# A mixture-of-experts inference step: blocks of gates issued every 1.875 steps instead of every 2

## The chip, the cores and the metric

The kernel runs on one core of one Trainium2 chip. The metric is the device time of one execution in microseconds, taken as the median of several runs.

## What is computed

One inference step of a small two-layer encoder, for 256 prompt rows and 128 sample rows of width 1024 (three tiles of 128 rows). Layer 0 mixes with a state-space block, layer 1 with windowed attention; behind each stands the same expert layer ("PEER"), and that layer is what the change touches:

```python
def block_fn(xb):                                  # 128 rows
    q = (xb @ w_q).reshape(128, 8, 256)            # 8 heads
    s1, s2 = q[..., :128] @ sub_k1.T, q[..., 128:] @ sub_k2.T
    # top 16 of each, top 16 of the sums: 128 experts a row, of 128 * 128
    eid  = e1 * 128 + e2
    gate = softmax(vs)
    act  = gelu(einsum('tkd,td->tk', u_tab[eid], xb))
    return einsum('tk,tkd->td', gate * act, v_tab[eid])
```

## The kernel before, in words

**The expert layer, dense for the prompt.** `peer(l)` runs twice, for layers 0 and 1. For the 256 prompt rows it doesn't fetch experts one by one. It multiplies the rows by all 128 x 128 experts, 128 at a time: `u_step(e2)` loads one tile of 128 experts, multiplies it with the rows into a PSUM bank, and ScalarE (ACT) writes the gelu of that into `G[e2 // 64][:, e2 % 64]`. `G[0]` and `G[1]` are the two halves of the experts' activations, 64 tiles of 128 x 256 numbers each. After 64 + 64 of these U steps come 128 V steps: `v_step(e2)` loads one tile of `p_v`, splits tile `e2` of `G`, and adds the product to four PSUM banks that stay open for all 128 steps. Full precision is made from pairs: `split` writes a rounded `hi` (a cast on ACT, L108) and the rest `lo` (a subtraction on VectorE, DVE, L109), and three matrix products replace one (L144 to L146 for U, L157 for V). For a V step the split of `G` has the names `phi` and `plo`. Some steps use the raw tile instead (L1199, L1246).

**Blocks of gates.** Before V may read a half of `G`, that half must be multiplied by the gates, which are nonzero only for chosen experts. `w_step(hf, t0)` (L1207) does it for 8 prompt rows and one half, all 64 tiles at once: DVE builds `ob` (L1212) and `og` (L1215); one tile `oa` is built by ACT (four L1225 and one L1226) and a second `oa` by DVE (L1228); TensorE (PE) multiplies 16 small matrices into a bank (L1232), 8 with the first `oa` and 8 with the second; DVE multiplies the half of `G` by that bank (L1234). 32 blocks make a half. Since each block touches every tile of its half, the first V step of a half needs all 32 blocks of it. `ob` and `og` have one buffer each, `oa` has two.

**Sample rows.** For the 128 sample rows the chosen experts are fetched: GpSimd (POOL) gathers rows of `p_u` into `gath`, DVE reduces each against the input (L1173, "U item"), and later PE multiplies gathered rows of `p_v` by small tiles `cm` (L1184 on DVE, L1190 on PE: a "quad", 8 matrix products of four gathered rows, 16 instructions in the profile).

**Order of the work.** Three loops of `peer` write the program down: 64 U steps of half 0; then 64 U steps of half 1 with the 32 blocks of half 0 among them; then 128 V steps, with the 32 blocks of half 1 among the first 64 of them. `tick` and `quads` add the U items and the quads by tables of due steps. The program is then put in order by a scheduler at build time, which fixes one sequence for each engine: an engine runs its sequence strictly in that order, and a semaphore wait holds up all that stands behind it. So the place where a line stands in the loops is a wish, and the built sequence decides. Casts of `hi` use a ring of two buffers, in the V steps of three (the third has the names `hix` and `lox`); a cast waits until PE has read the old contents of its buffer.

Of the kernel before, what the change touches and what calls it, by code (L numbers as in the profile page):

```python
# [61 lines left out]
def encoder_step(ctx: ExitStack, tc: tile.TileContext, t_in, t_out):  # L62
# [150 lines left out]
    def open_h():  # L213
        hold["pool"] = tc.tile_pool(name="resid", bufs=1, side="right")
        hold["h"] = T(hold["pool"].__enter__(), [P, NB, D], F32, tag="h")
        return hold["h"]
# [671 lines left out]
    def peer(l):  # L888
        with ExitStack() as c:
# [9 lines left out]
            HE = NKEY // 2  # L899
# [49 lines left out]
            def load_group(g):  # L949

                if g % 2:
                    xg[g] = (G[1][:, HE - 4:] if g == 1 else G[0][:, 32:36]).rearrange("p e t -> p (e t)")
                else:
                    xg[g] = T(one, [P, D], F32, tag="xg", bufs=1)
                rows = xrow[g].rearrange("c r d -> (c r) d")
                for q in range(GR):
                    pool.dma_start(xg[g][q * TG:(q + 1) * TG], rows)
# [236 lines left out]
            def u_step(e2):  # L1194
                ps = bank([P, NP])
                if e2 in NATIVE:
                    raw = load_raw(t_in["u_t"][l, e2])
                    for k in range(KD):
                        pe.matmul(ps, raw[:, k * P:(k + 1) * P], xf[:, k], start=(k == 0), stop=(k == KD - 1))  # L1199
                else:  # L1200
                    gemm_cols(ps, load_split(t_in["u_t"][l, e2]), xs[0], xs[1], 0, NP)
                act.activation(G[e2 // HE][:, e2 % HE], ps, AF.Gelu_apprx_tanh)
# [58 lines left out]
            def tick(s):  # L1261

                s0, n0 = start[0], 0
                for s1, n1 in U_DUE:
                    if s < s1:
                        break
                    s0, n0 = s1, n1
                want = P if s >= U_DUE[-1][0] else n0 + (n1 - n0) * (s + 1 - s0) // (s1 - s0)
                while done["u"] < want:
                    fetch_u(done["u"] + 2)  # L1270
                    u_item(done["u"])
                    done["u"] += 1
                    if due and due[0][0] <= done["u"]:
                        group_end(*due.pop()[1:])
                if due and done["u"] == P:
                    group_end(*due.pop()[1:])

            def quads(s):

                while done["v"] < 32 and V_DUE[done["v"]] <= s:  # L1280
                    v_quad(done["v"])
                    done["v"] += 1
                if s >= 2 * HE - 20 and done["f"] == 4 * V_FIRST and s < 2 * HE + 17:
                    return
                last = 4 * V_FIRST if s < 2 * HE else P
                ahead = 4 * done["v"] + (4 if s < 2 * HE else v_bufs(s))
                for _ in range(2):
                    if done["f"] < min(ahead, last):
                        fetch_v(done["f"], s)
                        done["f"] += 1  # L1290

            busy = True
            xs = [qhi, qlo]
            lent = tc.tile_pool(name="pe0", bufs=1)
# [34 lines left out]
            for e2 in range(HE):  # L1329
                u_step(HE + e2)  # L1330
                tick(HE + e2)
                if e2 % 2 == 1:
                    w_step(0, 8 * (e2 // 2))
                if e2 >= 7:
                    quads(HE + e2)
            xpool.__exit__(None, None, None)
# [4 lines left out]
            for e2 in range(2 * HE):  # L1341
                v_step(e2)
                if e2 == 35:
                    load_group(3)
                tick(2 * HE + e2)
                if e2 < HE and e2 % 2 == 1:
                    w_step(1, 8 * (e2 // 2))
                quads(2 * HE + e2)
                if e2 == 2 * HE - 7:
                    more.clear()  # L1350
                    lent.__exit__(None, None, None)
                    h = open_h()
                    pool.dma_start(h, spill)
# [16 lines left out]

    mamba(t_in["x"].rearrange("(b p) d -> p b d", p=P))
    peer(0)
    attention()
    peer(1)
    final()

# [95 lines left out]
```

## Time and profile before

| what | value |
|---|---|
| three runs | median 2511.06 us (2501.7 to 2518.12) |
| profiled execution, its own time | 2491.53 us |
| its span | 2489.0 us |
| PE busy | 2408.8 us, 97% of the span |
| DVE busy | 1883.5 us, 76% |
| ACT busy | 1244.5 us, 50% |
| mean granted TensorE clock | 0.99 |

Times in a trace count from the start of the span. The four places of this document are the ends of halves: in layer 0 the U steps of half 1 run from about 653 to 899 us and the V steps of half 0 from there to about 1137 us, in layer 1 from 1775 to 2018 and on to 2258 us. In a row of the timeline stand the start, the length, the engine, the line, the operation, output and inputs and the number of merged instructions, and in brackets the engine's idle time before it with what ended it. Matrix products overlap: the time that one takes from PE is the distance between two starts, not its length.

### The profile page before, as it was taken

The page shows a single profiled execution, that of the slowest core. Times are in us where ns is not written, and L with a number is a line of the kernel's source. Part 1 is how long each engine was busy: PE and PEld are TensorE (multiplying, and loading weights), DVE is VectorE, ACT ScalarE, POOL GpSimd, SP SyncE. Part 2 cuts the span into 40 slices and gives each one's busy share as a digit, 9 for nine tenths or more (in the row PEclk, how much of TensorE's full clock was granted, in tenths as well). Part 3 has the DMA queues.
Part 4 walks back from the last instruction along what each step waited for, and adds up shares of the span by engine and source line. Part 5 has one row for each costly group of instructions (what it writes and reads, how often), then busy time and mean ns, then how long its engine had stood idle before and what let it go on. Part 6 is the DMA issues. An engine that isn't in the chain of part 4 may idle for free.

```text
span 2489.0 us, 44541 instructions
## 1 busy us (share of the span) xinstructions
PE 2408.8 (97%) x16655; PEld 2017.4 (81%) x16656; DVE 1883.5 (76%) x4163; ACT 1244.5 (50%) x2406; POOL 727.3 (29%) x779
## 2 busy tenths in 40 slices
PE   8999999999999999999999998999999999999998
PEld 7899978999999986656666778999999986656676
DVE  5888846979988888777655675979988888777655
ACT  5656524433466665554344554433466665554343
POOL 2222200013334224446432100013334234346431
PEclk9999999999999999999999999999999999999999
DMA  5455434467789889989996424467799889989995
GB/s 198 169 183 180 163 125 145 143 234 253 277 313 350 297 299 342 328 323 392 363 339 201 142 69 162 137 229 262 274 311 355 297 299 343 328 325 388 362 336 206
DMA packets 177080, 649.76 MB, mean 261 GB/s; under 512 B 21136, under 2 KB 23040, under 8 KB 174208
## 3 DMA queue, kind: packets, MB, share of 16 engines
q1 hardware_dynamic: 99936, 365.85, 41.2%
q0 software_dynamic: 76928, 281.07, 31.5%
q8 instruction: 130, 2.13, 0.3%
q14 instruction: 86, 0.70, 0.1%
HBM read 630.62 MB, written 18.06 MB: 261 GB/s over the span
## 4 chain that ended last, share of the span: by engine, by line
PE 77%; DVE 4%; ACT 2%; issue 1%; DMA 1%; POOL 0%; POOLq 0%; ACTq 0%; DVEq 0%
PE bank L157 26%; PE bank L146 11%; PE bank L144 11%; PE bank L145 10%; PE bank L1190 5%; PE bank L1199 5%; PE bank L1246 3%; PE bank L1232 2%; DVE lo L109 2%; ACT hi L108 1%; DVE gath L1173 1%; PE bank L984 0%; PE bank L983 0%; DMA h<-hd 0%; PE bank L794 0%
## 5 line engine op out<-in xcount | busy, mean ns | idle before, releaser
L108 ACT CAST hi<-raw 128x1024 fp32r<-128x1024 f32 (+1 forms) x479 | 498.2, 1042 | 521.6 <-PE bank L145 380.6
L109 DVE TENSOR_TENSOR lo<-raw,hi 128x1024 fp32r<-128x1024 f32 (+1 forms) x479 | 581.8, 1216 | 193.8 <-ACT hi L108 192.2
L1133 POOL DMA_INDIRECT gath<-in_p_u,eidU x256 | 314.0, 1227 | 874.2 <-DVE gath L1173 468.6
L146 PE MATMUL bank<-xhi,lo 128*128 128x256 f32 (+1 forms) x1344 | 404.3, 301 | 6.4 <-DVE lo L109 6.4
L144 PE MATMUL bank<-xhi,hi 128*128 128x256 f32 (+1 forms) x1344 | 402.3, 300 | 0.0
L145 PE MATMUL bank<-xlo,hi 128*128 128x256 f32 (+1 forms) x1344 | 396.9, 295 | 0.0
L1133 POOL DMA_INDIRECT G<-in_p_v,eidT x256 | 290.7, 1135 | 303.4 <-PE bank L1190 220.6
L108 ACT CAST phi<-G 128x256 fp32r<-128x256 f32 x232 | 93.6, 406 | 362.1 <-PE bank L157 340.4
L146 PEld LDWEIGHTS bank<-xhi,lo 128*128 128x128 f32 x1344 | 253.8, 189 | 15.0 <-DVE lo L109 7.8
L144 PEld LDWEIGHTS bank<-xhi,hi 128*128 128x128 f32 x1344 | 253.8, 189 | 12.5 <-issue 6.9
L145 PEld LDWEIGHTS bank<-xlo,hi 128*128 128x128 f32 x1344 | 253.8, 189 | 0.3
L144 PE MATMUL bank<-qhi,hi 128*128 128x256 f32 (+1 forms) x792 | 243.9, 308 | 8.8 <-ACT xf L930 7.2
L146 PE MATMUL bank<-qhi,lo 128*128 128x256 f32 (+1 forms) x792 | 238.5, 301 | 1.9 <-DVE lo L109 1.9
L145 PE MATMUL bank<-qlo,hi 128*128 128x256 f32 (+1 forms) x792 | 238.6, 302 | 0.0
L109 DVE TENSOR_TENSOR plo<-G,phi 128x256 fp32r<-128x256 f32 x232 | 98.0, 424 | 163.1 <-PE bank L157 161.3
L157 PE MATMUL bank<-hi,phi 128*128 128x512 f32 x640 | 202.8, 412 | 13.7 <-ACT hi L108 7.9
L157 PE MATMUL bank<-lo,phi 128*128 128x512 f32 x640 | 204.9, 400 | 4.6 <-DVE lo L109 4.2
L157 PE MATMUL bank<-hi,plo 128*128 128x512 f32 x640 | 200.9, 395 | 0.0
L1225 ACT ACTIVATE oa<-ioh,e2T 128x128 f16<-128x128 f16 x512 | 163.6, 392 | 71.2 <-PE bank L1232 70.7
L157 PEld LDWEIGHTS bank<-hi,phi 128*128 128x128 f32 x640 | 117.2, 190 | 74.5 <-ACT hi L108 21.9
L1173 DVE SCALAR_TENSOR_TENSOR gath<-gath,xg 128x1024 f32<-128x1024 f32 x128 | 155.7, 1216 | 9.6 <-DMA gath<-in_p_u,eidU 9.6
L1173 DVE SCALAR_TENSOR_TENSOR gath<-gath,G 128x1024 f32<-128x1024 f32 x128 | 155.8, 1220 | 8.9 <-DMA gath<-in_p_u,eidU 8.8
(361 smaller groups left out, 4918.4 us busy)
## 6 DMA issues: line engine op xcount, KB each, us to landing
raw<-in_u_t SPq DMA_DIRECT2D x256, 512.0 KB
raw<-in_p_v SPq DMA_DIRECT2D x256, 512.0 KB
raw<-in_w_in SPq DMA_DIRECT2D x32, 512.0 KB
raw<-in_p_w_q SPq DMA_DIRECT2D x32, 512.0 KB
raw<-in_w_z SPq DMA_DIRECT2D x16, 512.0 KB
s<-in_state_ssm SPq DMA_DIRECT2D x8, 1024.0 KB
out_sm_ssm<-s SPq DMA_DIRECT2D x8, 1024.0 KB
raw<-in_w_out SPq DMA_DIRECT2D x16, 512.0 KB
```

What stands on the lines that cost most here:

```text
L108: act.copy(hi, raw)
L109: dve.tensor_tensor(lo, raw, hi32, op=OP.subtract)
L144: pe.matmul(ps, whi[:, s], xhi[:, k, c0:c1], start=(k == 0), stop=False)
L145: pe.matmul(ps, whi[:, s], xlo[:, k, c0:c1], start=False, stop=False)
L146: pe.matmul(ps, wlo[:, s], xhi[:, k, c0:c1], start=False, stop=(k == KD - 1))
L157: mm = pe.matmul(ps, x, w[:, hf * n:(hf + 1) * n], start=s_, stop=e_)
L1133: pool.indirect_dma_start(out=tile_, out_offset=None, in_=tab, in_offset=bass.IndirectOffsetOnAxis(ap=idx, axis=0))
L1173: pin(dve.scalar_tensor_tensor(tile_, tile_, 1.0, xg[g], op0=OP.mult, op1=OP.mult, accum_out=au[g][:, j:j + 1]))
L1190: pin(pe.matmul(out_s[hf][32 * q:32 * q + 32, :], cm[:, q], rows[q][:, hf * 512:hf * 512 + 512], start=(r == 0), stop=(r == 31), tile_posi ...
L1199: pe.matmul(ps, raw[:, k * P:(k + 1) * P], xf[:, k], start=(k == 0), stop=(k == KD - 1))
L1225: act.activation(a[:, i], ioh, AF.Square, scale=-1.0, bias=e2T[:, t, 0:1])
L1246: pe.matmul(accs[b][hf], G[e2 // HE][:, e2 % HE, b * P:(b + 1) * P], raw[:, hf * 512:hf * 512 + 512], start=False, stop=False)
```

## The change

The blocks stood at every second step: block i at step 2i + 1 of its 64 steps, the last at step 63. Now block i stands at step 1 + floor(1.875 i): 1, 2, 4, 6, 8, 10, 12, 14, 16, 17, 19, and so on to 55, 57, 59. The last block of half 0 so stands four U steps earlier, that of half 1 four V steps earlier. No instruction is added or taken away.

```diff
+            w_at = {1 + (60 * i) // 32: 8 * i for i in range(32)}
             busy = True
...
             for e2 in range(HE):
                 u_step(HE + e2)
                 tick(HE + e2)
-                if e2 % 2 == 1:
-                    w_step(0, 8 * (e2 // 2))
+                if e2 in w_at:
+                    w_step(0, w_at[e2])
...
                 tick(2 * HE + e2)
-                if e2 < HE and e2 % 2 == 1:
-                    w_step(1, 8 * (e2 // 2))
+                if e2 in w_at:
+                    w_step(1, w_at[e2])
                 quads(2 * HE + e2)
```

What the scheduler made of it is shown for three places of layer 0. In layer 1 the same sequences stand.

**PE, at the end of half 1's blocks.** `oa` numbers tell the blocks apart, L157 is a V step, L1190 a quad. Between two rows shown stand further instructions of the same block or quad only. Before:

```order
L157 MATMUL bank_10548<-hi_12949,plo_12954 128x512
L1232 LDWEIGHTS oa_12806
...
L1190 MATMUL bank_7292<-G_620_3971,cm_12831 32x512 x4
L1232 LDWEIGHTS oa_12897
...
L1232 LDWEIGHTS oa_12977
...
L157 MATMUL bank_10545<-hi_13004,phi_13008 128x512
```

And now:

```order
L157 MATMUL bank_10548<-hi_12979,plo_12984 128x512
L1232 LDWEIGHTS oa_12482
...
L1232 LDWEIGHTS oa_12571
...
L1232 LDWEIGHTS oa_12637
...
L1232 LDWEIGHTS oa_12714
...
L1190 MATMUL bank_7292<-G_620_3971,cm_12739 32x512 x4
L1232 LDWEIGHTS oa_12805
...
L1232 LDWEIGHTS oa_12866
...
L1190 MATMUL bank_7292<-G_620_3971,cm_12891 32x512 x4
L157 MATMUL bank_10545<-hi_13004,phi_13008 128x512
```

Before, blocks 30, 31 and 32 and one quad stood between the last V product of half 0 (`plo_12954`) and the first of half 1 (`phi_13008`). Now blocks 27 to 32 and two quads stand there: three blocks and a quad have moved behind the last V step of half 0.

**DVE, in the same place, now.** `ob`, `og`, `oa` and `G` are the parts of blocks, L109 `lo` belongs to a V step of half 1, L1173 is a U item.

```order
L1234 SCALAR_TENSOR_TENSOR G_1193_7286<-bank_12477,G_1193_7286 128x64x8
L1215 TENSOR_TENSOR og_12569<-ob_12567,g_617_3965 128x1024
L1228 TENSOR_TENSOR oa_12585<-ioh_76,e2T_3964 128x512
L109 TENSOR_TENSOR lo_13064<-raw_13061,hi_13063 128x1024
L1212 TENSOR_TENSOR ob_12633<-ioh_76,e1T_3963 128x512
L1234 SCALAR_TENSOR_TENSOR G_1193_7286<-bank_12566,G_1193_7286 128x64x8
L1215 TENSOR_TENSOR og_12635<-ob_12633,g_617_3965 128x1024
L1228 TENSOR_TENSOR oa_12651<-ioh_76,e2T_3964 128x512
L1173 SCALAR_TENSOR_TENSOR gath_12925,au_12185<-gath_12925,G_620_3971 128x1024
L1212 TENSOR_TENSOR ob_12710<-ioh_76,e1T_3963 128x512
```

So one `lo` stands between the parts of blocks 28 and 29, one U item between those of 29 and 30; in the same way another U item (L1173) stands between the G of block 31 and the `og` of block 32, all of it now behind the last V step on PE. On ACT a cast, `hi_13063`, stands ahead of the `oa` of block 28.

**ACT, at the end of half 0's blocks.** Here `hi_10573` is the cast for V step 1, L1202 the gelu of the last U step, `phi_10555` the first split of V step 0. Before:

```order
L1225 ACTIVATE oa_10601<-ioh_76,e2T_3964 128x128 x4
L1226 ACTIVATE oa_10601<-oa_10601 128x512
L108 CAST hi_10573<-raw_10571 128x1024
L1202 ACTIVATE G_1193_7286<-bank_10473 128x256
L108 CAST phi_10555<-G_620_3971 128x256
```

And now:

```order
L108 CAST hi_10551<-raw_10549 128x1024
L1202 ACTIVATE G_1193_7286<-bank_10468 128x256
L108 CAST hi_10573<-raw_10571 128x1024
L1202 ACTIVATE G_1193_7286<-bank_10503 128x256
L108 CAST phi_10555<-G_620_3971 128x256
```

The parts of a block have gone from the rows above; the last three rows stand as before.

## Prediction

> **What bounds the kernel now.** I read the page's first and fourth parts, then the busy times by stage, then PE's waits, then the timeline at the four ends of halves, then the granted clock there.
>
> ```profile
> PE 2408.8 (97%) x16655; PEld 2017.4 (81%) x16656; DVE 1883.5 (76%) x4163; ACT 1244.5 (50%) x2406; POOL 727.3 (29%) x779
> PE 77%; DVE 4%; ACT 2%; issue 1%; DMA 1%; POOL 0%; POOLq 0%; ACTq 0%; DVEq 0%
> core 0: us, PE busy (x) PEld busy (x) DVE busy (x) ACT busy (x) POOL busy (x), PEclk, DMA share, GB/s
> 653.00:899.00 246.00, 243.39 (x2359) 228.43 (x2357) 209.23 (x329) 159.09 (x316) 87.23 (x81) 1.00 0.89 312
> 899.00:1137.03 238.03, 230.83 (x1401) 153.93 (x1401) 188.50 (x321) 131.84 (x265) 103.83 (x89) 1.00 0.90 328
> ```
>
> PE is the bound: 97% busy, 77% of the chain that ended last. So this change, which leaves every instruction in place, can act only through PE's idle time and clock. The last two rows are the two stages with blocks of layer 0: PE idles 2.6 of 246 us in the first and 7.2 of 238 in the second. Those of layer 1 are their twins. This is what PE waits for in the second (line, what it waited for, us, times, longest):
>
> ```profile
> PE bank L157 <- ACT phi L108: 3.0, 2, 1.6
> PE bank L1232 <- ACT oa L1226: 1.9, 1, 1.9
> PE bank L157 <- ACT hi L108: 1.0, 1, 1.0
> PE bank L1232 <- DVE og L1215: 0.8, 2, 0.5
> ```
>
> Two waits on `phi` open the two halves of V, and the 1.9 us on `oa` is a wait between the last two blocks. So something does stand still at both ends of halves; the question is what.
>
> **End of half 0: removes nothing.**
>
> ```profile
> 898.71 0.28 PE L146 MATMUL bank<-xhi,lo 128*128 128x256 f32 x1
> 900.58 0.73 PE L157 MATMUL bank<-hi,phi 128*128 128x512 f32 x2 [1.59 <-ACT phi L108]
> 896.84 0.69 DVE L1234 SCALAR_TENSOR_TENSOR G<-bank,G 128x512 f32<-128x512 f32 x1
> 898.91 1.04 ACT L108 CAST hi<-raw 128x1024 fp32r<-128x1024 f32 x1 [0.26 <-PE bank L145]
> 899.86 0.38 ACT L1202 ACTIVATE G<-bank 128x256 f32<-128x256 f32 x1
> 900.14 0.70 ACT L108 CAST phi<-G 128x256 fp32r<-128x256 f32 x2
> ```
>
> The last block had multiplied `G` by 897.5, 1.2 us before PE even finished its last U step. PE then idles 1.59 us for `phi`, and `phi` is late because ACT has a cast and a gelu ahead of it, and the cast waits for PE (L145) to let go of a `hi` buffer. In the changed sequence cast, gelu and `phi` stand in the same order. Moving the blocks forward doesn't touch this: 0 us, bounds 0 (same order) to a gain of 1.6 us a layer (if `phi` were free).
>
> Inside the U stage the blocks now come at 1 or 2 steps' distance. DVE was busy 209.2 of 246 us there and does about 1.9 us for a block (steps of 0.34, 0.60, 0.60 and 0.34 us between starts, as in the rows below); 32 blocks in 60 steps instead of 64 leave it under 90%. A late `lo` cost PE no more than the 2.6 us of all its idle time in that stage. I take 0, bounds -1 to +2 us a layer.
>
> **End of half 1: the tail grows.** Layer 0, then layer 1:
>
> ```profile
> 1129.67 0.64 PE L1232 MATMUL bank<-og,oa 128*128 128x64 f16 x16
> 1130.24 1.92 PE L1190 MATMUL bank<-G,cm 128*32 128x512 f32 x16
> 1132.51 0.63 PE L1232 MATMUL bank<-og,oa 128*128 128x64 f16 x16 [0.34 <-DVE og L1215]
> 1135.00 0.64 PE L1232 MATMUL bank<-og,oa 128*128 128x64 f16 x16 [1.86 <-ACT oa L1226]
> 1137.03 1.22 PE L157 MATMUL bank<-hi,phi 128*128 128x512 f32 x2 [1.39 <-ACT phi L108]
> 1133.00 1.28 ACT L1225 ACTIVATE oa<-ioh,e2T 128x128 f16<-128x128 f16 x4
> 1132.02 1.03 ACT L108 CAST hi<-raw 128x1024 fp32r<-128x1024 f32 x1
> 1133.17 0.69 DVE L1234 SCALAR_TENSOR_TENSOR G<-bank,G 128x512 f32<-128x512 f32 x1 [0.26 <-PE bank L1232]
> 1133.78 0.68 DVE L1215 TENSOR_TENSOR og<-ob,g 128x1024 f16<-128x1024 f16 x1
> 1134.38 0.42 DVE L1228 TENSOR_TENSOR oa<-ioh,e2T 128x512 f16<-128x512 f16 x1
> 1134.71 1.22 DVE L109 TENSOR_TENSOR lo<-raw,hi 128x1024 fp32r<-128x1024 f32 x1
> 1135.85 0.69 DVE L1234 SCALAR_TENSOR_TENSOR G<-bank,G 128x512 f32<-128x512 f32 x1
> ...
> 2256.41 0.94 PE L1232 MATMUL bank<-og,oa 128*128 128x64 f16 x16 [1.86 <-ACT oa L1226]
> 2258.57 1.22 PE L157 MATMUL bank<-hi,phi 128*128 128x512 f32 x2 [1.22 <-ACT phi L108]
> ```
>
> Blocks 30, 31, 32 and a quad run here with no V step between: 7.36 us from 1129.67 to 1137.03. Two neighbouring blocks cannot come closer than a chain: PE reads the first `oa`; 0.49 us after the block's start ACT begins the next one (1132.51 to 1133.00); 2.00 us later PE starts (1135.00). Period 2.49 us, of which PE works 0.57 (1129.67 to 1130.24). A V step between two blocks would hide it.
>
> In the built sequence the change does the opposite of its wish: six blocks, 27 to 32, and two quads now stand behind half 0's last V step. Counting from block 27's start, with the sequences shown:
>
> - 27 to 28: ACT first casts `hi_13063`, whose buffer PE frees only with that last V step: about 0.1 us, 0.98 for the cast (1132.02 to 1133.00), 2.00 for `oa`: 3.1 us.
> - 28 to 29: ACT's chain, 2.5 us (DVE's `lo` of 1.14 us just fits).
> - 29 to 30: DVE's chain. After its `oa` for block 28, at 2.3 us, it must do `lo` 1.14, `ob` 0.34, G 0.60, `og` 0.60, `oa` 0.33, a U item 1.15, `ob` 0.34, G 0.60, `oa` 0.33, `og` 0.60: 8.4 us; block 30 starts then, 2.85 after block 29.
> - 30 to 31: 2.5, the quad between is covered.
> - 31 to 32: G 0.66 us after the block's start, 0.61, the U item 1.15, `og` 0.60, `oa` 0.42: 3.5 us.
> - 32 to the first V product: the block's 0.57 and a quad of 1.86; `phi`, 2.03 us behind the block before (1135.00 to 1137.03), is covered: 2.45 us.
>
> The U item and the quad have their lengths from these rows:
>
> ```profile
> 1137.76 1.21 DVE L1173 SCALAR_TENSOR_TENSOR gath<-gath,G 128x1024 f32<-128x1024 f32 x1
> 1138.91 0.08 DVE L1173 DVE_READ_ACCUMULATOR gath<-gath,G 128x1 f32 x1
> 1141.43 0.62 PE L157 MATMUL bank<-hix,phi 128*128 128x512 f32 x2
> 1144.31 1.92 PE L1190 MATMUL bank<-G,cm 128*32 128x512 f32 x16
> 1146.17 0.74 PE L157 MATMUL bank<-hi,phi 128*128 128x512 f32 x2
> ```
>
> Sum: 16.9 us. PE did three of those blocks and one quad earlier before, among V steps, at 3 x 0.57 + 1.86 = 3.6 us, so the stage ends 16.9 - 7.4 - 3.6 = **5.9 us later** a layer. Bounds: 4 us (all at 2.49: 5 x 2.49 + 2.45 - 11.0) to 8 us (each period with a further 0.4 us of DVE work).
>
> **The clock.** The same place in windows of 3.41 us; the column behind the busy times is the granted clock:
>
> ```profile
> 1133.62:1137.04 3.42, 0.66 (x17) 0.54 (x17) 2.95 (x6) 1.76 (x6) 2.75 (x2) 0.99 1.03 419
> 1137.04:1140.45 3.41, 3.41 (x8) 2.73 (x9) 3.41 (x7) 0.55 (x2) 1.88 (x2) 0.51 1.03 410
> 2253.16:2256.57 3.41, 1.19 (x25) 0.70 (x22) 3.14 (x8) 3.17 (x7) 2.14 (x3) 1.00 1.02 410
> 2256.57:2259.99 3.42, 2.20 (x19) 1.79 (x17) 2.90 (x5) 1.02 (x3) 2.53 (x2) 0.50 1.04 418
> 2259.99:2263.40 3.41, 3.41 (x9) 2.64 (x8) 2.00 (x5) 0.41 (x1) 1.88 (x2) 0.50 1.02 405
> 898.10:901.52 3.42, 1.83 (x12) 1.49 (x11) 3.02 (x5) 3.16 (x6) 0.00 (x0) 1.00 0.82 260
> ```
>
> A window in which PE works 0.66 or 1.19 us is followed by one at half speed; one with 1.83 is not; and once at half, 2.20 us were too few to come back. Twelve V products took 4.40 us in layer 0 (1137.03 to 1141.43) against 2.88 for the next twelve: 1.5 us lost, and about 2.5 in layer 1, with its slower block. So 4.0 us are paid now. The longer tail fills five windows, most with one block each: half clock from the second on. One of the two quads then takes twice 1.86 (+1.9), the start of V loses about 2.0, and two periods grow by 0.3 (0.94 against 0.64 for a block): 4.5 us a layer. Bounds: 0, and 8.7 (both quads 3.7, five periods 1.5, two windows of V 3.4). Change: 2 x 4.5 - 4.0 = +5.0 us.
>
> The Trainium skill (TensorE: Matmul & The Clock Gate, "Part 1: The HAM clock gate") gives half clock after one or more idle windows of about 3.4 us. The window's length agrees with the trace; but no window here was idle, and the clock fell all the same, so the measurement decides.
>
> **Sum.** 2 x 5.9 + 5.0 = 16.8, say 17 us. Against its own time, the profiled execution's 2491.5 us (span 2489.0) becomes 2508.5. The runs' median is 2511.06, 19.5 us higher; the same 17 us on it give **2528 us**, +0.7%. Beyond 1% is about what can be told from no change here.
>
> **Rivals.**
>
> *The waits vanish, as the change's place suggests* (faster). The blocks wait for nothing of the V steps, so DVE and ACT might be through with them early. For it: DVE and ACT idle 50 and 106 us in that stage. Against it: PE's sequence holds six blocks behind the last V step, and two buffers of `oa` keep each next one back. If it held, 1.6 us at each of two half ends, 3.6 and 3.1 us at the others (0.34 + 1.86 + 1.39 and 1.86 + 1.22) and 4.0 us of clock would go: -14 us, 2497.
>
> *Half clock through the whole tail* (slower by more). For it: 2.20 us of work did not bring the clock back. Against it: a quad fills half a window by itself, and a full one did. Price: 2 x 5.9 + 2 x 8.7 - 4.0 = +25 us, 2536; it decides from the second quad being at half speed in both layers.
>
> *Full clock through it.* For it: two of the five windows hold a quad, 1.86 us, more than the 1.83 that kept the clock at half 0's end. Against it: the others hold one or two blocks, 0.6 to 1.1 us, and 1.19 was too little. Price: 11.8 - 4.0 = +8 us, 2519. By the rule of the Trainium skill named above this would be the case.
>
> *The tail costs little*, as the V steps ahead of it shed the waits on `hi` and `og` outside the half ends (1.0 and 0.5 us a layer are all there is of them) and the clock stays full. For it: fewer blocks stand among those steps. Against it: PE then reaches the tail earlier and finds ACT and DVE no further. Price: 2 x (5.9 - 1.5) - 4.0 = +5 us, 2516.
>
> **How the numbers follow.** Forecast 58%; waits vanish 7%; half clock throughout 17%; full clock 12%; little cost 6%. The range holds the forecast, both clock cases and a share of the little-cost case, with some 7 us for the median itself, as the three runs differ by 16: 2508 to 2544. Faster by over 1% would need 25 us, more than the rival's whole gain: 0.02. Slower by over 1% takes half of the half-clock case and a bit of the forecast's upper side: 0.14. Within 1%: 0.84.
>
> **What would show it.** Right: six L1232 groups in a row at 2.5 to 3.5 us distance ahead of half 1's first V product, PE idle about 10 us in that stretch instead of 3.6, waiting on ACT `oa` and DVE `og`; half clock there in two or more windows a layer; 1.6 us on `phi` at half 0's end unchanged; the stage of half 0's blocks at 246 us within 2. Wrong: fewer than five blocks in the tail, distances under 2.4, or a first V product of half 1 in layer 0 before 1137.

## The result, and the profile after

The changed kernel took 2541.65 us (median of four runs, 2537.54 to 2544.24) against 2508.05 us for the kernel before: a ratio of 1.0121, 95% interval 1.0101 to 1.0141, so 33.6 us more, twice the 17 of the forecast. That lies within the range of the prediction (2508 to 2544), 13.7 us above its forecast of 2528, and on the side to which it had given a chance of 0.14. The profiled execution took 2543.42 us, its span is 2541.7.

First the page and the busy times of the two stages with blocks of layer 0 (the same columns as before; the stage of half 0's blocks now ends at 914.40, that of half 1's at 1162.12):

```profile
PE 2420.3 (95%) x16655; PEld 2030.2 (80%) x16656; DVE 1881.9 (74%) x4163; ACT 1245.6 (49%) x2406; POOL 710.6 (28%) x779
653.00:914.40 261.40, 247.93 (x2357) 232.29 (x2355) 209.60 (x329) 159.45 (x316) 84.43 (x81) 0.98 0.86 293
914.40:1162.12 247.72, 233.15 (x1401) 156.38 (x1401) 189.72 (x320) 133.02 (x266) 95.51 (x86) 0.97 0.88 316
```

The work is the same to the instruction. The second stage grew from 238.0 to 247.7 us, as announced. The first, to which the prediction gave 0 us, grew from 246.0 to 261.4: PE's idle time there rose from 2.6 to 13.5 us, its busy time by 4.5, as the granted clock fell to 0.98. What PE waited for: first stage before and now, then second stage now:

```profile
PE bank L146 <- DVE lo L109: 1.8, 4, 0.6
...
PE bank L146 <- DVE lo L109: 8.7, 11, 2.8
PE bank L144 <- ACT hi L108: 1.4, 2, 0.8
...
PE bank L1232 <- DVE og L1215: 10.7, 4, 3.5
PE bank L1232 <- ACT hi L108: 2.3, 1, 2.3
PE bank L157 <- ACT phi L108: 1.6, 1, 1.6
```

The tail at the end of half 1, layer 0, and the first V product of half 0:

```profile
915.96 0.73 PE L157 MATMUL bank<-hi,phi 128*128 128x512 f32 x2 [1.59 <-ACT phi L108]
...
1139.84 0.65 PE L1232 MATMUL bank<-og,oa 128*128 128x64 f16 x16 [2.29 <-ACT hi L108]
1143.98 1.01 PE L1232 MATMUL bank<-og,oa 128*128 128x64 f16 x16 [3.49 <-DVE og L1215]
1146.99 1.01 PE L1232 MATMUL bank<-og,oa 128*128 128x64 f16 x16 [2.00 <-DVE og L1215]
1150.34 1.01 PE L1232 MATMUL bank<-og,oa 128*128 128x64 f16 x16 [2.34 <-DVE og L1215]
1151.28 3.52 PE L1190 MATMUL bank<-G,cm 128*32 128x512 f32 x16
1154.73 0.64 PE L1232 MATMUL bank<-og,oa 128*128 128x64 f16 x16
1158.28 1.01 PE L1232 MATMUL bank<-og,oa 128*128 128x64 f16 x16 [2.90 <-DVE og L1215]
1159.22 2.96 PE L1190 MATMUL bank<-G,cm 128*32 128x512 f32 x16
1162.12 0.73 PE L157 MATMUL bank<-hi,phi 128*128 128x512 f32 x2
```

Six blocks in a row and two quads, as foretold, 22.3 us long instead of 16.9; the 1.59 us wait on `phi` stands as it stood. The same place in windows of 3.41 us, the granted clock behind the busy times:

```profile
1137.46:1140.87 3.41, 0.75 (x17) 0.56 (x16) 3.41 (x6) 2.15 (x3) 1.14 (x1) 1.00 1.02 413
1140.87:1144.29 3.42, 0.31 (x7) 0.34 (x8) 3.42 (x7) 2.59 (x6) 0.00 (x0) 0.50 0.99 382
1144.29:1147.70 3.41, 1.42 (x28) 1.28 (x26) 3.41 (x6) 1.93 (x6) 0.00 (x0) 0.50 0.99 372
1147.70:1151.11 3.41, 1.07 (x21) 0.94 (x19) 2.92 (x7) 1.96 (x6) 0.93 (x1) 0.50 0.40 101
1151.11:1154.52 3.41, 3.41 (x21) 0.68 (x18) 1.96 (x4) 1.82 (x5) 0.00 (x0) 0.50 0.27 108
1154.52:1157.94 3.42, 0.85 (x20) 0.52 (x16) 2.53 (x5) 1.91 (x5) 2.57 (x2) 1.00 0.31 56
1157.94:1161.35 3.41, 3.07 (x28) 1.48 (x32) 2.08 (x6) 1.02 (x3) 2.50 (x4) 0.50 0.81 284
1161.35:1164.76 3.41, 3.41 (x20) 2.18 (x13) 2.73 (x6) 0.37 (x1) 2.72 (x3) 1.00 0.91 314
```

Five windows at half speed, with both quads in them. A quad all but fills its window and the next one is at full speed: behind the second quad the first V products of half 1 run at full speed here, where they began at half speed before.

What had not been foretold is best seen at the second block of half 0, the place of the longest wait on `lo`. First DVE's rows there, then GpSimd's, then PE's:

```profile
684.03 1.24 DVE L109 TENSOR_TENSOR lo<-raw,hi 128x1024 fp32r<-128x1024 f32 x1
688.46 0.69 DVE L1234 SCALAR_TENSOR_TENSOR G<-bank,G 128x512 f32<-128x512 f32 x1 [3.19 <-PE bank L146]
689.06 0.68 DVE L1215 TENSOR_TENSOR og<-ob,g 128x1024 f16<-128x1024 f16 x1
689.66 0.42 DVE L1228 TENSOR_TENSOR oa<-ioh,e2T 128x512 f16<-128x512 f16 x1
690.00 1.22 DVE L109 TENSOR_TENSOR lo<-raw,hi 128x1024 fp32r<-128x1024 f32 x1
...
684.01 0.96 POOL L1133 DMA_INDIRECT G<-in_p_v,eidT  x1 [0.31 <-issue]
685.28 0.94 POOL L1133 DMA_INDIRECT G<-in_p_v,eidT  x1 [0.30 <-issue]
686.52 0.94 POOL L1133 DMA_INDIRECT G<-in_p_v,eidT  x1 [0.30 <-issue]
...
684.77 0.64 PE L1232 MATMUL bank<-og,oa 128*128 128x64 f16 x16
691.27 0.58 PE L146 MATMUL bank<-xhi,lo 128*128 128x256 f32 x1 [2.83 <-DVE lo L109]
```

The block's sixteen products end at 685.41 and DVE has been free since 685.27, but DVE begins `G` only at 688.46. In the program `G` waits for nothing but these sixteen products. The trace's record of semaphore events shows the signal of the last of them at 688.43, 3.0 us behind its row; usually it comes 0.2 us after the product's start. `og`, `oa` and `lo` stand behind `G` in DVE's sequence, and PE waits for that `lo`. I call this a late signal. In the first profile of the kernel before no `G` begins more than 0.3 us behind the later of its products and DVE's last instruction; here, among half 0's blocks, 6 of 32 do in layer 0 (blocks 2, 8, 12, 15, 18 and 21, 15.6 us together) and 5 in layer 1 (the same without 12). The row's "releaser" says L146: it is inferred, and names the instruction of PE that happened to end then.

Half 1's blocks have such waits too, 7 in each layer, of 1.5 us at most but for one: that of block 26 in layer 0, just ahead of the tail.

```profile
1137.26 0.69 DVE L1234 SCALAR_TENSOR_TENSOR G<-bank,G 128x512 f32<-128x512 f32 x1 [5.91 <-remote]
```

The products of block 26 end at 1130.53, and the event of their signal stands at 1137.24 ("remote": the profile names nothing that ended the wait). ACT is held up as well as DVE: its `oa` for block 27 waits, of other engines' work, only for the eighth product of block 26, whose row ends at 1130.30, and begins at 1132.99. So it is not DVE that is slow here; what comes late is PE's signal.

### The profile page after: what moved, and what is told of

It is laid out like the page before. It is cut to its first block, busy times and chain, and to the rows that moved or that the text cites. A ratio compares the mean times of both kernels' runs of the same rounds, so it can differ in the third digit from the quotient of the medians.

```text
span 2541.7 us, 44555 instructions
## 1 busy us (share of the span) xinstructions
PE 2420.3 (95%) x16655; PEld 2030.2 (80%) x16656; DVE 1881.9 (74%) x4163; ACT 1245.6 (49%) x2406; POOL 710.6 (28%) x779
## 5 line engine op out<-in xcount | busy, mean ns | idle before, releaser
L109 DVE TENSOR_TENSOR lo<-raw,hi 128x1024 fp32r<-128x1024 f32 (+1 forms) x479 | 580.2, 1213 | 189.5 <-ACT hi L108 182.3
L1133 POOL DMA_INDIRECT gath<-in_p_u,eidU x256 | 308.4, 1205 | 953.0 <-DVE gath L1173 537.2
L146 PE MATMUL bank<-xhi,lo 128*128 128x256 f32 (+1 forms) x1344 | 408.9, 304 | 18.7 <-DVE lo L109 18.6
L144 PE MATMUL bank<-xhi,hi 128*128 128x256 f32 (+1 forms) x1344 | 407.4, 304 | 0.6 <-ACT hi L108 0.6
L1133 POOL DMA_INDIRECT G<-in_p_v,eidT x256 | 281.1, 1098 | 284.1 <-PE bank L1190 206.4
L146 PEld LDWEIGHTS bank<-xhi,lo 128*128 128x128 f32 x1344 | 258.6, 192 | 27.0 <-DVE lo L109 22.0
L144 PEld LDWEIGHTS bank<-xhi,hi 128*128 128x128 f32 x1344 | 258.4, 192 | 13.4 <-ACT hi L108 5.9
L144 PE MATMUL bank<-qhi,hi 128*128 128x256 f32 (+1 forms) x792 | 243.5, 308 | 8.1 <-ACT xf L930 6.5
L146 PE MATMUL bank<-qhi,lo 128*128 128x256 f32 (+1 forms) x792 | 238.1, 301 | 1.9 <-DVE lo L109 1.9
L145 PE MATMUL bank<-qlo,hi 128*128 128x256 f32 (+1 forms) x792 | 238.1, 301 | 0.0
L157 PE MATMUL bank<-lo,phi 128*128 128x512 f32 x640 | 202.8, 398 | 8.3 <-DVE lo L109 8.2
L157 PE MATMUL bank<-hi,phi 128*128 128x512 f32 x640 | 202.0, 407 | 7.1 <-ACT phi L108 4.2
L157 PE MATMUL bank<-hi,plo 128*128 128x512 f32 x640 | 201.9, 397 | 0.0
L109 DVE TENSOR_TENSOR plo<-G,phi 128x256 fp32r<-128x256 f32 x232 | 97.6, 423 | 129.1 <-PE bank L157 111.5
L1173 DVE SCALAR_TENSOR_TENSOR gath<-gath,G 128x1024 f32<-128x1024 f32 x128 | 155.8, 1218 | 45.5 <-DMA gath<-in_p_u,eidU 43.0
L1234 DVE SCALAR_TENSOR_TENSOR G<-bank,G 128x512 f32<-128x512 f32 x128 | 88.0, 687 | 111.3 <-PE bank L1232 61.7
L157 PEld LDWEIGHTS bank<-hi,phi 128*128 128x128 f32 x640 | 116.7, 188 | 66.9 <-issue 19.8
```

Source lines behind the costliest of these rows:

```text
L109: dve.tensor_tensor(lo, raw, hi32, op=OP.subtract)
L144: pe.matmul(ps, whi[:, s], xhi[:, k, c0:c1], start=(k == 0), stop=False)
L145: pe.matmul(ps, whi[:, s], xlo[:, k, c0:c1], start=False, stop=False)
L146: pe.matmul(ps, wlo[:, s], xhi[:, k, c0:c1], start=False, stop=(k == KD - 1))
L157: mm = pe.matmul(ps, x, w[:, hf * n:(hf + 1) * n], start=s_, stop=e_)
L1133: pool.indirect_dma_start(out=tile_, out_offset=None, in_=tab, in_offset=bass.IndirectOffsetOnAxis(ap=idx, axis=0))
```

## The experiments

Each ran beside the kernel before on the same chip; the ratio is to that. Stages are counted in the traces from the first block of half 0 to the first V product of half 0 (A), from there to the first V product of half 1 (B), and from there to the last V product (C), in us for layer 0 / layer 1:

| kernel | median | before, same chip | ratio, 95% interval | A | B | C |
|---|---|---|---|---|---|---|
| before, first profile | 2508.05 | | | 219.6 / 219.6 | 236.4 / 236.6 | 220.7 / 221.9 |
| changed | 2541.65 | 2508.05 | 1.0121 (1.0101 to 1.0141) | 235.3 / 234.1 | 246.2 / 246.9 | 221.6 / 224.8 |
| e1 before again | 2502.03 | 2504.75 | 0.9988 (0.9975 to 1.0001) | 221.1 / 223.1 | 238.0 / 238.0 | 219.6 / 220.5 |
| e2 half 0 only | 2511.84 | 2504.75 | 1.0035 (1.0021 to 1.0049) | 225.8 / 225.7 | 238.2 / 238.1 | 222.4 / 221.7 |
| e3 half 1 only | 2527.84 | 2504.75 | 1.0105 (1.0084 to 1.0125) | 223.0 / 220.5 | 245.6 / 245.6 | 224.9 / 224.4 |
| e4 even steps | 2543.00 | 2504.75 | 1.0168 (1.0146 to 1.0190) | 235.0 / 235.0 | 242.7 / 242.5 | 225.2 / 226.0 |
| e5 changed, plain rows | 2497.62 | 2491.99 | 1.0025 (1.0009 to 1.0041) | 216.9 / 216.8 | 243.5 / 243.7 | 217.0 / 219.1 |
| e6 before, plain rows | 2492.59 | 2491.99 | 1.0002 (0.9987 to 1.0016) | 219.4 / 219.3 | 237.2 / 238.3 | 220.4 / 221.2 |
| e7 half 1, dense start | 2507.95 | 2491.99 | 1.0073 (1.0046 to 1.0099) | 219.6 / 219.6 | 236.9 / 238.7 | 228.5 / 228.6 |
| e8 changed again | 2548.18 | 2511.97 | 1.0146 (1.0124 to 1.0168) | 230.3 / 230.5 | 245.8 / 245.4 | 223.4 / 224.6 |
| e9 changed, plain, again | 2500.70 | 2511.97 | 0.9949 (0.9931 to 0.9968) | 216.9 / 216.9 | 244.1 / 245.6 | 218.4 / 218.9 |
| e10 half 0 only, again | 2520.38 | 2511.97 | 1.0031 (1.0021 to 1.0040) | 229.8 / 230.9 | 239.0 / 238.2 | 221.0 / 221.8 |
| e11 half 0 only, G behind lo | 2503.89 | 2500.09 | 1.0016 (0.9999 to 1.0032) | 221.8 / 224.8 | 238.4 / 237.4 | 221.9 / 222.0 |
| e12 before, G behind lo | 2493.79 | 2500.09 | 0.9974 (0.9962 to 0.9986) | 218.6 / 218.3 | 238.0 / 238.0 | 221.3 / 222.0 |

**e1: the kernel before once more.**

> The kernel before, unchanged, profiled a second time. Its first profile (2491.5 us) lay below every one of its timed runs (2501.7 to 2518.1), so the comparison of the two traces may mix two things. Theory A, the change's order alone costs the time: the second profile lies again at 2490 to 2495 us, the stage of half 0's blocks (first block to first V product of half 0) takes 219.6 us in both layers, G (L1234) never waits more than 0.3 us once its block's last product is done. Theory B, part of the loss in that stage is not the order but PE's signals that reach DVE and ACT late, in some executions of any of the two kernels: the second profile lies at 2500 to 2518, the stage takes 222 to 232 us, and G waits 1 us or more behind a finished block here too.

The second profile's span is 2492.3 us, near the first's 2489.0, and stage A sits between what the two theories said. The order before has late signals too: `G` was late at blocks 8 and 14 of layer 0 (1.3 us each) and at 8, 11 and 14 of layer 1. One of them:

```profile
732.85 0.56 PE L1232 MATMUL bank<-og,oa 128*128 128x64 f16 x13
...
734.74 0.69 DVE L1234 SCALAR_TENSOR_TENSOR G<-bank,G 128x512 f32<-128x512 f32 x1 [1.40 <-PE bank L1232]
```

So the first profile of before, on which the prediction was built, had shown an execution without them. By itself that explains 1.5 and 3.5 of the 15 us a layer.

**e2 and e3: each half alone.** The table of steps is used for one loop, the old one for the other:

```diff
+            w_old = {1 + 2 * i: 8 * i for i in range(32)}
...
-                if e2 in w_at:
-                    w_step(1, w_at[e2])
+                if e2 in w_old:
+                    w_step(1, w_old[e2])
```

This is e2; in e3 the same exchange is made at `w_step(0, ...)` instead.

> The new spacing for the blocks of half 0 alone; half 1's blocks stand at every second V step as before. Theory A (order): the stage of half 0's blocks takes 235 us a layer as in the changed kernel, the end of half 1 stays as before (three blocks and a quad between the halves' V products, about 7.4 us), so +30 us on the kernel before, about 2538. Theory of the prediction (only the end of half 1 costs): no change, 2508 within 6. Theory B (late signals): between 2508 and 2540, and the places at which G waits differ from those in the changed kernel.

> The new spacing for the blocks of half 1 alone; half 0's blocks stand as before. The prediction's own term alone: five or six blocks behind half 0's last V step, +8 us a layer (5.9 of waits and 2.5 of clock), about 2525. Theory A: the same +8 to +10 us a layer, 2525 to 2530, with the stage of half 0's blocks at 219.6 us. Theory B: the same tail, but the stage of half 0's blocks at 222 us or more in this kernel too, though its order there is the order before.

Half 0 alone costs 7.1 us, half 1 alone 23.1; the sum is 30 of the 33.6. The prediction had 0 and 17. For e2 "no change" falls and so does "235 us a layer": up to the first V steps the sequences of e2 and of the changed kernel are the same on all engines, and yet A took 226 us in one and 235 in the other, with the late `G`s at the same blocks (2, 8, 15, 18, 21), only shorter in sum (10.0 us against 15.6 in layer 0). So the order goes far to decide where a signal can be late, and something else how late it is. In e3, B grew by 7.6 us a layer, near the 8.4 that the prediction had put there; C grew by 4 to 5, where it had nothing.

**e4: distance or place.**

```diff
-            w_at = {1 + (60 * i) // 32: 8 * i for i in range(32)}
+            w_at = {2 * i: 8 * i for i in range(32)}
```

> Blocks at every second step as before, but at the even steps (0, 2, ... 62), so each one step earlier; no two blocks closer than 2 steps. It separates the distance between blocks from their place in the steps. If the closer distance costs the time in the stage of half 0's blocks, that stage takes 219.6 us again and only the end of half 1 changes (four blocks behind half 0's last V step instead of three: +2 to +4 us a layer), 2512 to 2518. If the place in the steps costs it (a block that now meets other instructions of DVE), the stage takes 225 to 235 us although the distance is unchanged, and the time lies at 2520 to 2540.

Stage A took 235.0 us in both layers with the old distance of 2. A closer distance is therefore not what costs the time there. Six `G`s a layer were late, by 0.9 to 3.8 us (blocks 2, 8, 11, 14, 17, 20), and PE waited on `lo` and `og` behind them. B grew by 4.6 us a layer.

**e5 and e6: the row fetches as plain DMAs.** In all kernels so far the late signals of half 0's blocks fall where GpSimd issues gathers, nearly always several one behind the other, as in the rows above. The edit leaves every sequence of PE, ACT, GpSimd and SyncE as it was and fetches 128 successive rows of the table, of the same size, instead of the chosen experts' rows, so it leaves out the sample rows' choice of experts:

```diff
-                pool.indirect_dma_start(out=tile_, out_offset=None, in_=tab,
-                                        in_offset=bass.IndirectOffsetOnAxis(ap=idx, axis=0))
+                pool.dma_start(tile_, tab[128 * (n_names[0] % 128):128 * (n_names[0] % 128) + 128, :])
```

> The changed kernel, but GpSimd fetches the rows of the sample side with plain DMAs of the same size from its own queue in place of the indirect gathers, so these rows are not the chosen experts' (128 rows in a row of the table); the sequences of PE, ACT, GpSimd and SyncE are instruction for instruction those of the changed kernel. Theory L (PE's signals reach DVE and ACT late while GpSimd issues an indirect gather): no G (L1234) waits more than 0.3 us behind its finished block, the stage of half 0's blocks takes 219 to 223 us a layer instead of 234 to 235, the end of half 1 keeps most of its loss, so the time is about 25 us below the changed kernel's 2541.65, at 2510 to 2520. Rival (the order itself, or the traffic of the row fetches, makes these waits): the late G's stay, the stage takes 226 to 235 us, the time stays at 2530 to 2542.

> The kernel before with the same plain row fetches. Theory L: 2489 to 2495 us, stages of half 0's blocks at 219.6 us in both layers, the ones of half 1's blocks at 236.5, as in its first profile, in which no signal was late; so the changed kernel with plain fetches less this one gives the cost of the order alone, by the prediction +17 (+12 to +25). Rival: as the kernel before, 2502 to 2508, with late G's at blocks 8, 11 and 14.

Not one `G` was late in either, and e5 came out faster than any theory had said (2497.62 us, for 2510 to 2520 by Theory L). A took 216.9 us in the changed order, 2.5 less than in the order before. The changed kernel with plain fetches is 5.0 us slower than the one before with plain fetches (2497.62 against 2492.59), not the 17 of the prediction. But the kernel before, with its gathers, also took 2492 on that chip, and e7 beside it had no late signal although it gathers. So these two did not yet tell whether the gathers mattered.

**e7: fewer blocks behind the last V step.** Against the kernel before; half 0's blocks stay where they were:

```diff
+            w_new = {}
+            for i in range(32):
+                w_new.setdefault(max(i, 2 * i - 3), []).append(8 * i)
...
-                if e2 < HE and e2 % 2 == 1:
-                    w_step(1, 8 * (e2 // 2))
+                for t0 in w_new.get(e2, ()):
+                    w_step(1, t0)
```

> Half 0's blocks as before; half 1's blocks at steps max(i, 2i - 3): 0, 1, 2, 3, 5, ... 59, so the last one four V steps ahead, as in the change, and the distance 2 from the fourth on. In the built sequence two blocks stand behind half 0's last V step (before: three and a quad; in the change: six and two quads). Theory of the prediction (what counts is how many blocks stand behind the last V step): the stage from the first V product of half 0 to that of half 1 takes 232 to 235 us a layer against 238 in the repeated kernel before and 246 in the change, so about 2496 to 2502. Rival (blocks that end earlier cost by themselves, by taking DVE and ACT from the V steps): 242 to 246 us, about 2525.

Neither came: B took 236.9 and 238.7 us, about as before, but C 228.5 instead of some 221, so 7 to 8 us a layer were paid behind the tail, for a reason that was not followed, and the kernel is 0.73% slower. Counting blocks behind the last V step is thus not enough to forecast a kernel.

**e8, e9 and e10: changed, plain and half 0 alone, on one chip.**

> The changed kernel, unchanged, once more, beside the kernel before on the same chip. In the last three runs no G (L1234) waited behind a finished block, with gathers (the dense-start kernel) or without, and the kernel before took 2492 there instead of 2502 to 2508: so late signals may belong to the chip or the session as much as to the gathers. Theory S (the chip's state decides whether PE's signals come late, and the change only exposes them): where no signal is late, the changed kernel takes 5 us more than the kernel before (216.9 instead of 219.4 us for half 0's blocks, 243.5 instead of 237.5 to the first V product of half 1, 217 to 219 instead of 221 behind it); where they are late, some 30 us more, with G late at blocks 2, 8, 15, 18, 21 again. Theory of the prediction: 17 us more in both cases. Theory O (the order alone makes the loss): about 33 us more in any case.

> The changed kernel with plain row fetches (other rows than the chosen experts') once more, beside the changed kernel on the same chip. Theory L (gathers bring the late signals): if the changed kernel beside it has late G's, this one has none, and is about 25 us faster than it. Theory S without gathers: if the changed kernel has late G's, this one has them too and the two are within 5 us. If neither has any, the two are within 5 us and the runs decide nothing between L and S.

> The new spacing for half 0's blocks alone, once more, on the chip of the two runs before. From the stages of the plain kernels: where no signal is late, half 0's blocks take 2.5 us a layer less and nothing else changes, 5 us below the kernel before (faster by 0.2%); where signals are late, 5 us a layer more, 7 us above it as the first time.

This chip had late signals, and the three settle that the gathers bring them; which part of a gather does, they don't show. With gathers the changed kernel takes 2548.18 us, with plain fetches 2500.70: 47.5 us less, and no `G` late. Theory L had said about 25, so it holds in kind and not in size. It is more than the 33.6 us of the change because the kernel before loses by late signals too: it took 2511.97 us beside these runs, against 2491.99 on the chip of e5 to e7, where putting plain fetches into it changed nothing (e6). The same block 2 in both, first with gathers (DVE, the three GpSimd rows, PE), then with plain fetches:

```profile
691.04 0.69 DVE L1234 SCALAR_TENSOR_TENSOR G<-bank,G 128x512 f32<-128x512 f32 x1 [3.16 <-PE bank L146]
...
686.62 0.97 POOL L1133 DMA_INDIRECT G<-in_p_v,eidT  x1 [0.30 <-issue]
687.90 0.94 POOL L1133 DMA_INDIRECT G<-in_p_v,eidT  x1 [0.30 <-issue]
689.14 0.94 POOL L1133 DMA_INDIRECT G<-in_p_v,eidT  x1 [0.30 <-issue]
...
687.39 0.64 PE L1232 MATMUL bank<-og,oa 128*128 128x64 f16 x16
693.86 0.58 PE L146 MATMUL bank<-xhi,lo 128*128 128x256 f32 x1 [2.81 <-DVE lo L109]
```

```profile
684.26 0.69 DVE L1233 SCALAR_TENSOR_TENSOR G<-bank,G 128x512 f32<-128x512 f32 x1 [0.25 <-PE bank L1231]
...
682.24 1.07 POOL L1133 DMA_DIRECT2D G<-in_p_v  x2
...
683.58 0.64 PE L1231 MATMUL bank<-og,oa 128*128 128x64 f16 x16
```

3.01 us from the end of the block's products to `G` in the one, 0.04 in the other (its line numbers are one lower). Of the instructions of PE that signal between 640 and 1160 us of e8, quads left out, 29 of the 127 whose signal was due while GpSimd issued a gather had no event within 0.75 us, and 11 of the other 271; in e9 none of 407. e10 took the same 230 us in A as the changed kernel beside it: same order, same chip, same stage. It was 8.4 us slower than before, as e2 had been 7.1.

**e11 and e12: G behind the next lo.** If a late signal costs time because `lo` stands behind `G`, then `G` need only step back. In the stage of half 0's blocks the multiplication of a block is written one block later and kept in program order with `lo`:

```diff
-            dve.tensor_tensor(lo, raw, hi32, op=OP.subtract)
+            low = dve.tensor_tensor(lo, raw, hi32, op=OP.subtract)
+            if pinned[0]:
+                pin(low)
...
-                dve.scalar_tensor_tensor(gv, ps.rearrange("p t e -> p e t"), 1.0 / GSCALE, gv, op0=OP.mult, op1=OP.mult)
+                held.append((gv, ps))
+                if hf:
+                    flush(0)
...
+            def flush(keep):
+                while len(held) > keep:
+                    gv, ps = held.pop(0)
+                    mul = dve.scalar_tensor_tensor(gv, ps.rearrange("p t e -> p e t"), 1.0 / GSCALE, gv, op0=OP.mult, op1=OP.mult)
+                    if pinned[0]:
+                        pin(mul)
...
+                flush(1)
                 if e2 in w_at:
                     w_step(0, w_at[e2])
```

> The new spacing for half 0's blocks alone, and on DVE in that stage each block's G (L1234) is kept behind the next lo, one block later, so that the lo which PE needs next no longer stands behind a wait on PE. From the built sequences: between the end of a block's products and the moment at which PE needs the lo behind its G there were 0.2 to 0.9 us to spare for 24 of 32 blocks, now at least 6 for 31 of 32. Theory L (late signals cost time because G holds up lo): half 0's blocks take 217 to 221 us a layer on any chip, against 226 to 231 without this where signals were late; the time is that of the kernel before or up to 8 us below it (ratio 0.997 to 1.000). Rival (PE waits on lo because DVE has too much to do, or the late signal holds up the casts on ACT as well): 225 us or more where signals are late, 5 to 10 us above the kernel before.

> The kernel before (both halves at every second step) with the same edit for half 0's blocks: G behind the next lo. Theory L: half 0's blocks take 218 to 220 us a layer on any chip (221 to 223 where signals were late, 219.6 where not), so 0 to 6 us below the kernel before (ratio 0.9975 to 1.000), nearer 0 on a chip without late signals. Rival: no change or slower, since the held bank and the later G take more than the few late signals of this order cost.

Both traces still have late signals: in stage A it is now `og`, which takes a buffer that PE has read, that begins up to 2.7 us late, at 3 places in layer 0 and 2 in layer 1 of e11, and at 3 in each layer of e12. But PE waits less behind them. What PE waits for in stage A of layer 0 in e10, then in e12 (there L149 is the U product with `lo`):

```profile
PE bank L146 <- DVE lo L109: 6.0, 7, 2.9
PE bank L1232 <- DVE og L1215: 1.3, 1, 1.3
```

```profile
PE bank L149 <- DVE lo L110: 2.3, 3, 1.8
```

e12 is faster than the kernel before by 0.26% (0.14 to 0.38), with A at 218.6 and 218.3 us: the one version here that computes all of it and beats the kernel before. That is little: the same kernel twice differed by 0.12% (e1), and the profiled execution of e12, 2502.54 us, was the slowest of its seven, so the stages of its trace are not those of its median. e11 brought A to 221.8 and 224.8 us, above the 217 to 221 of its theory, below the rival's 225, and to no measurable difference from before. So the place of `G` seems to explain most of the loss in A and not all, as far as A can be compared between chips: the new spacing without this edit (e2 and e10, 226 to 231 us) ran on others. Three waits on `lo` of 3.7 us in all were left in layer 0 of e11, and what holds them up was not followed further.

## Why the prediction was right and wrong, step by step

**End of half 0, 0 us: right.** The wait on `phi` is 1.59 us before and after.

**Inside the U stage, "I take 0, bounds -1 to +2 us a layer": this is the step that failed.** The order alone even gains 2.5 us a layer (e5 against e6, one chip), beyond the lower bound; with late signals the profiled pair shows +15.7 and +14.5. I had argued from averages: DVE under 90% busy, PE idle for 2.6 us. Neither is a margin. The margin lies in DVE's sequence and can be worked out from rows that the prediction had: behind block 2's products PE has 24 U products (22 and the next step's first two) until it needs the `lo` that stands behind this `G`, at 0.118 us from start to start 2.83 us; `G`, `og`, `oa` and `lo` take 0.60, 0.60, 0.33 and 1.14, so 2.67. That leaves 0.16 us. A signal 3.01 us late (e8) must then cost 3.01 - 0.16 = 2.85 us; PE waited 2.81.

In the changed order 24 of half 0's 32 blocks have under 1 us to spare in this sense, in the order before 23: the margin was hardly changed. What changed is which blocks end while gathers are issued, and no sequence on PE, DVE or ACT alone tells that; the profile of before had no late signal to point at it. Their number hardly changed (8 blocks of layer 0 against 7), but their place in a run of gathers issued one behind the other did. In layer 0 blocks 2, 8 and 21 of the changed kernel end 2.7 to 3.4 us into such a run and are 2.4 to 3.2 us late; in e1 blocks 11 and 20 end 7.0 us into theirs and are 0.2 us late at most. Block 14 of e1 and block 15 of the changed kernel both end 6.2 us into a run of five and are 1.3 and 1.5 us late. The place doesn't settle all of it: block 12 ends 6.2 us into a run in both layers and is 2.5 us late in one alone.

**The tail, +5.9 us: right in place, in count and, by a balance of errors, in size.** Distances between the starts, forecast, in the changed kernel, and in e9 without late signals:

| | 27 to 28 | 28 to 29 | 29 to 30 | 30 to 31 | 31 to 32 | 32 to V | sum |
|---|---|---|---|---|---|---|---|
| forecast | 3.1 | 2.5 | 2.85 | 2.5 | 3.5 | 2.45 | 16.9 |
| changed, layer 0 | 4.14 | 3.01 | 3.35 | 4.39 | 3.55 | 3.84 | 22.3 |
| e9, layer 0 | 3.14 | 2.50 | 5.62 | 4.52 | 3.35 | 4.06 | 23.2 |

Where the chains ran as supposed they were right to 0.15 us (3.14, 2.50, 3.35). Three things were not priced. Both quads ran at half speed and were no longer covered: 30 to 31 and 32 to V took 2.0 and 1.6 us more, for which the clock term held 1.9 together. And the U item between blocks 29 and 30 had to wait for its rows, since the tail now comes before they have landed (DVE in e9; in layer 1 of the changed kernel it waited 4.24 us, and 29 to 30 took 7.7):

```profile
1122.30 0.42 DVE L1227 TENSOR_TENSOR oa<-ioh,e2T 128x512 f16<-128x512 f16 x1
1125.29 1.23 DVE L1172 SCALAR_TENSOR_TENSOR gath<-gath,G 128x1024 f32<-128x1024 f32 x1 [2.57 <-DMA gath<-in_p_u]
```

The third is a late signal, in the runs with gathers: the 1.0 us by which 27 to 28 is longer in the changed kernel comes from DVE, which is behind with its work since block 26's late `G`. The tail begins later for it too: PE waits 2.29 us ahead of block 27, whose `og` DVE can only build at 1139.01; by then the rows for the U item between 29 and 30 had landed in this layer. Against all that, the V steps ahead of the tail took 220.9 us in e9 against 229.1 in e6: 8.2 less, where the moved work accounts for 3.6. Of the rest, 2.0 us is what PE idled there before; 2.6 us I can't name. B in all: +6.3 and +5.4 us without late signals (e5 against e6; +6.9 and +7.3 with e9), +6.8 and +7.2 on e8's chip (against e10), for a forecast of 5.9 + 2.5 = 8.4.

**The clock, +2.5 us a layer: half speed came, in another place.** Half speed lasted 13.7 to 17.1 us of the tail, four or five windows (five in both layers of the changed kernel), but PE has little to do in them beside the quads. The 2.0 us that I let the start of V lose were not lost here: the quad ahead of it brings the clock back, as the window at 1161.35 shows. In e5 C is 3.4 and 2.1 us shorter than in e6. By the rule of the Trainium skill that the prediction had weighed (TensorE: Matmul & The Clock Gate, "Part 1: The HAM clock gate") the tail would have stayed at full clock; it did not.

**The sum, +17: half 1 alone measured +23.1 (e3).** Without late signals the whole order costs 5 us by the medians of e5 and e6; the stages of their two profiles make it 0.4 and 0.8 us a layer (-2.5 + 6.3 - 3.4 and -2.5 + 5.4 - 2.1), those of e9 and e6 2.4 and 2.6. The other 28 or so of the 33.6 come only where PE's signals are late. In stages, with gathers less plain fetches on the same chip (e8 less e9): A +13.4 and +13.6, B +1.7 and -0.2, C +5.0 and +5.7, 39 us of the 47.5. So a forecast near the time was carried by the wrong parts: 17 us of order where there were 5, and nothing for the signals. That the time fell into the range is luck to that extent; on the chip of e8 the same kernel took 2548.18 us, outside of it.

**The rivals.** "Half clock through the whole tail" (2536) lay nearest to the number, and half clock there was; but the 4.2 us a layer by which it lay above the forecast were not in B, which without late signals came out below the forecast. "The tail costs little" had the right direction for the V steps ahead of it. "The waits vanish" and "full clock" fell. None held what happened in stage A.

**The profiled execution.** I had moved the sum from the profiled 2491.5 to the median of the runs, 19.5 us higher, without asking what those were. On the chip where the one trace with gathers (e7) had no late signals the kernel before takes 2491.99 us, on the others 2500 to 2512: the profile of before was a run without late signals, of a kernel whose other runs seem mostly to have them. That they explain the 19.5 us is not shown: e1's profile has late signals and took 2494.03, and the runs of e5, without gathers, differ by 17 us among themselves. But it was the trace's one hint, and I used it as an offset.

Left open: what in a gather makes PE's signals late, why on one chip or in one run and not in another, and whether the products themselves end late or only their signals. A row's end on PE is modelled: the Trainium skill (Perfetto Trace Analysis, "Tensor Engine Instruction (MATMUL, LD_WEIGHTS)") says that the time until a product's signal is seen lies outside of its slice. The trace agrees, with 3.0 us between the row's end and the event at block 2.

## What to carry to other kernels

Before calling an engine's idle time a margin, work out at each wait how long the waiting instruction may be late until the first instruction behind it, on its own engine, is missed elsewhere: here it was 0.2 to 0.9 us at 24 of 32 blocks, on an engine that was idle for 15% of the stage. Keep instructions that wait for another engine behind those which that engine will need next; one reordering of this kind gave 0.26% without touching the work. And when the profiled run is faster than every timed run, look for what the others have before adding the difference.

## What the runs showed of the hardware

- While GpSimd issues indirect gathers, signals of PE can reach DVE up to 5.9 us late (`G` of block 26 of half 1, changed kernel, layer 0; 3.8 us among half 0's blocks) and ACT 2.7 us (`oa` of block 27 there), against 0.04 us from the modelled end of the products to `G` where none is late. With plain DMAs from the same queue, in the same sequences of PE, ACT, GpSimd and SyncE and on the same chip, none was over 0.75 us late (e9).
- How often this happens depends on the chip or the run: the same kernel before had medians of 2491.99, 2500.09, 2504.75 and 2511.97 us beside the four groups of experiments, while the changed kernel with plain fetches took 2497.62 and 2500.70 beside the lowest and the highest of these.
- Half clock, tail of the changed kernel: 3.07 and 3.41 us of PE work in a window at half speed brought full speed back in the next, 1.07 and 1.42 did not; 0.85 us in a window at full speed was followed by half speed.
